# A hybrid decoder block on one core: 22 pairs of raw expert products ahead of the expert stage instead of 12, with the gate work in four pieces beside them

## The chip, the cores and the metric

The kernel runs on one core of one Trainium2 chip. The metric is device time in microseconds of one execution. Engines are named as in the profile: PE is TensorE, DVE is VectorE, ACT is ScalarE, POOL is GpSimd, SP is SyncE; PEld is the weight load of TensorE.

## What is computed

One decoder block for 256 tokens of width 2048, all in float32: adaLN modulation, two token mixers in parallel (sparse attention and an S5 state space), a merge, and then the expert mixer, in which most of the time goes. Cut to what the change touches:

```
mod = silu(c) @ ada_w + ada_b                # 6 parts of 2048: sh1, sc1, g1, sh2, sc2, g2
...
bu = einsum(u, bb)                           # S5: 64 groups of 16 channels drive a state of 64
x_re, x_im = associative_scan(...)           # y from the states
...
x  = x + g1 * (mixed @ w_out)
h2 = rms_norm(x) * (1 + sc2) + sh2
q  = h2 @ w_q                                # 8 heads, two halves of 128
s1, s2 = q @ sub_keys                        # top 16 of 128 twice, then top 16 of the sums
expert, gate = 16 of 16384 experts per head and token, softmax of their scores
x  = x + g2 * sum over (gate * gelu(h2 . u_tab[expert])) * v_tab[expert]
out = rms_norm(x) * final_g
```

The expert mixer is computed densely: h2 is multiplied with all 16384 rows of u, the result is multiplied with a gate matrix that is zero where an expert is not chosen, and that product is multiplied with all of v.

## The kernel before

All large matrix products are done three times over halves: `load_split` (L95 to L101) reads a block of 128x1024 into `st` (5 buffers, SP's queue), rounds it on ACT into `hi` (3 buffers) and subtracts on DVE into `lo` (3 buffers); PE multiplies hi with both halves of the other operand and lo with the first half. One such load is the unit of the whole kernel: one `st` transfer, one `hi` on ACT, one `lo` on DVE, 24 matmuls of 256 columns (or 12 of 512) on PE.

The program is written as one stream, and a scheduling layer places the instructions in fixed order on each engine. Work beside the main stream is put in with `tick`, which is called once for each load of `pair_T` and `cols_t`: it runs items of lists that have a first and a last load (`during`), and items of the list `later`, each with a cost in credits. A tick adds `credit[1]` (RATE, 2.0) to what is left of the credit, of which it keeps at most 2.0, and runs items from the head of `later` while the credit covers their cost:

```
credit[0] = min(credit[0], 2.0) + credit[1]
while later and later[0][0] <= credit[0]:
```

The stages in order are: the projections and mixers (to about 850 us), the second normalisation, and then from 882 us on, the part that the change is about:

- **Top-k scores.** Eight heads: a product of h2 with four blocks of w_q (`pair_T`), scores against the sub-keys (L1004), and top-k items into `later` (`top16`, `topk_head`, `topk_ranks`, `index`; L988 to L1062). Beside them `last` runs the final four column blocks of the adaLN matrix on PE (L222), one load per tick.
- **Raw products** (`u_raw`, L1144 on): a pair of expert blocks, 4 loads, 96 matmuls (L512 to L514), then a gelu in two ACT and two DVE instructions (L1149 to L1152) into an `xs` buffer (17 of them). `lead` = 12 pairs run before the gates exist.
- **Gates** (`gate_step`, L1109 on): 16 steps of 16 tokens. A step is four DVE instructions on 128x2048 (L1118 a comparison, L1120 twice a product, L1122 a comparison), 32 matmuls (L1128) and four ACT copies into `stage` (L1129). Two steps fill a chunk, which POOL's queue writes to `gt_dram`. `gate_step` costs 4.5 credits. What is left of `later` after the 12 pairs runs in a loop (L1229).
- **Expert stage**: 16 groups (q) of 8 expert blocks. `gate_load` reads a group's gates back (`gm`, 3 buffers, POOL's queue). `u_fin` multiplies raw values with them (L1159) and splits the result into `wcat` (3 buffers of four blocks, L104 and L105). `v_cols` (4 per group) multiplies with four blocks of v: 48 matmuls of 512 columns (L1180 to L1182), 64 `v_cols` in all. The other 52 pairs of raw products stand between them: two beside the `v_cols` of a group and two after its last.
- **End**: modulation by g2, residual, norm, output.

Two places further ahead are touched as well. `s5_state` (L578) starts each of 32 states with two products of 32 rows into one bank of PSUM (L590); `compress` (L673) multiplies 128 columns that are taken at a step of 8 (L682). PSUM has two banks named `mm` and six named `ps`.

Of the kernel before, what the change touches and what calls it, by code (L numbers as in the profile page):

```python
# [39 lines left out]
T8 = 2048 + 16  # L40
# [14 lines left out]
RATE = 2.0  # L55
# [17 lines left out]
def hybrid_block(ctx: ExitStack, tc: tile.TileContext, i: dict, out: bass.AP):  # L73
# [54 lines left out]
    pool = pa.enter_context(tc.tile_pool(name="pa", bufs=1))  # L128

    def t8(shape, name, dtype=F32):  # L130
        n = math.prod(shape[1:])
        t = pool.tile([P, T8], dtype, name=name, tag="t8", bufs=10)[:, :n]
        if len(shape) == 2:
            return t
        names = "abc"[:len(shape) - 1]
        return t.rearrange(f"p ({' '.join(names)}) -> p {' '.join(names)}", **dict(zip(names, shape[1:])))
# [420 lines left out]
    s5_out = {}  # L557

# [19 lines left out]
    def s5_state(b):  # L578

        cb, r = b // 4, b % 4  # L580
        if r == 0:
            if cb + 1 < 8:
                make_table(cb + 1)
            s5_mats(cb)
            s5_ps[cb] = ps_bank([P, SEQ])
        bst = s5_mat[cb][0]
        bu = ps2()
        sl = slice(32 * r, 32 * r + 32)
        for c in range(2):
            PE.matmul(bu[:, c], bst[sl, c, :], uT[sl, cb, :], start=True, stop=True)  # L590
# [82 lines left out]
    def compress(kind):  # L673
        xc = xcs[kind]
        pts = [ps_bank([P, P]) for _ in range(2)]
# [286 lines left out]
    NXS = 17  # L962
# [103 lines left out]
    last = [step for j in range(20, 24) for step in ada_steps(j, pl=tk)]  # L1066
    during(loads[0], loads[0] + 4 * PH, last)
# [6 lines left out]
    ada_row(1, 80, tk)  # L1074
# [28 lines left out]
    later.append((4.0, softmax))  # L1103
# [5 lines left out]
    def gate_step(t0):  # L1109

        if "stage" not in gpool:
            gpool["stage"] = pg.enter_context(tc.tile_pool(name="gp2", bufs=1))
        c, z = t0 // GT, t0 % GT
        if z == 0:
            chunk[c] = gpool["stage"].tile([P, NBLK, GT], F32, name="stage", bufs=2)
        ts = slice(t0, t0 + TG)
        o1 = gp.tile([P, 2, P, TG], HF, name="o1", bufs=2)
        V.tensor_tensor(o1[:, 0], iota_b, idxT[:, 0, None, ts].to_broadcast([P, P, TG]), op=OP.is_equal)  # L1118
        for part in (1, 0):
            V.tensor_mul(o1[:, part], o1[:, 0], gate2[:, part, None, ts].to_broadcast([P, P, TG]))  # L1120
        o2 = gp.tile([P, TG, P], HF, name="o2", bufs=2)
        V.tensor_tensor(o2, iota_r[:, None, :].to_broadcast([P, TG, P]),  # L1122
# [111 lines left out]
    for q in range(2):  # L1234
        gate_load(q)
# [132 lines left out]
```

## Time and profile before

| | |
|---|---|
| median of 3 runs (lowest, highest) | 2552.22 us (2546.16, 2557.81) |
| the profiled execution | 2554.16 us, of it 2552.1 us span |
| mean granted TensorE clock | 0.981 |
| busy: PE, DVE, ACT, POOL | 96%, 65%, 46%, 3% |
| HBM | 526.12 MB read, 23.12 MB written |

Busy shares are means over stages with different limits, and a pipelined matmul counts as busy from its issue to its modelled end, so a PE at 96% is not one at its peak. The pitch of its matmuls (the distance of two starts) tells more. In the slices of the page the span is cut into 40 pieces of 63.8 us; a digit is the busy share in tenths.

### The profile page before, as it was taken

How to read it: one execution, taken by the hardware profiler on the slowest of the kernel's cores; microseconds unless marked ns; L12 is line 12 of the kernel's file. 1: busy time of each engine (PE TensorE's matmuls, PEld its weight loads, DVE VectorE, ACT ScalarE, POOL GpSimd, SP SyncE). 2: the span in 40 equal slices, each digit the busy share in tenths (PEclk: the TensorE clock that was granted, in tenths of full speed). 3: DMA queues.
4: the chain of work that ended last, by engine and by line, in shares of the span. 5: the costliest groups of instructions: out<-in, count | busy, mean ns of one | idle time of the engine just before them, and what ended most of it. 6: DMA issues, size and time to landing. Idle time of an engine off the chain costs nothing.

```text
span 2552.1 us, 42825 instructions
## 1 busy us (share of the span) xinstructions
PE 2448.5 (96%) x17410; PEld 2127.0 (83%) x17410; DVE 1668.6 (65%) x2690; ACT 1176.5 (46%) x1527; POOL 65.1 (3%) x117
## 2 busy tenths in 40 slices
PE   7999999999999999995599999999999999999997
PEld 4787787777898788995488999999899999989996
DVE  4559767886555579959555665666666566665666
ACT  4444524645534534456444444444444444444444
POOL 0000200000000000000100000000000000000000
PEclk9999999999999999996799999999999999999999
DMA  9965666666777677554756665665666566565554
GB/s 347 376 227 176 225 202 210 214 199 209 281 264 255 211 237 253 188 186 173 298 197 192 211 198 197 203 208 191 203 206 207 192 204 206 191 207 189 190 191 139
DMA packets 149761, 552.03 MB, mean 216 GB/s; under 512 B 16748, under 2 KB 20492, under 8 KB 147133
## 3 DMA queue, kind: packets, MB, share of 16 engines
q1 hardware_dynamic: 135200, 493.08, 57.1%
q0 software_dynamic: 8928, 40.17, 4.4%
q10 hardware_dynamic: 5436, 16.06, 1.8%
q8 instruction: 136, 2.23, 0.4%
q14 instruction: 61, 0.49, 0.1%
HBM read 526.12 MB, written 23.12 MB: 215 GB/s over the span
## 4 chain that ended last, share of the span: by engine, by line
PE 57%; DVE 5%; DMA 2%; ACT 1%; issue 1%; DVEq 0%; POOL 0%; POOLq 0%; ACTq 0%
PE mm L512 10%; PE mm L513 10%; PE mm L514 10%; PE ps L1182 9%; PE ps L1180 9%; PE ps L1181 9%; DVE o L1120 1%; DVE o L1122 1%; DMA st<-in_peer_w_q_dram 1%; DVE lo L100 1%; DVE o L1118 1%; DMA gm<-gt_dram 0%; ACT hi L98 0%; PE ps L1004 0%; DMA gt_dram<-stage 0%
## 5 line engine op out<-in xcount | busy, mean ns | idle before, releaser
L100 DVE TENSOR_TENSOR lo<-st,hi 128x1024 fp32r<-128x1024 f32 x738 | 902.2, 1223 | 667.9 <-ACT hi L98 666.8
L98 ACT ACTIVATE hi<-st 128x1024 fp32r<-128x1024 f32 x738 | 781.4, 1060 | 1120.3 <-PE mm L513 430.5
L512 PE MATMUL mm<-cat,hi 128*128 128x256 f32 x2832 | 804.1, 284 | 0.6 <-ACT cat L104 0.6
L513 PE MATMUL mm<-cat,hi 128*128 128x256 f32 x2832 | 793.8, 280 | 1.0 <-DVE cat L105 0.9
L514 PE MATMUL mm<-cat,lo 128*128 128x256 f32 x2832 | 792.8, 280 | 0.0
L512 PEld LDWEIGHTS mm<-cat,hi 128*128 128x128 f32 x2832 | 533.6, 188 | 33.4 <-issue 26.5
L514 PEld LDWEIGHTS mm<-cat,lo 128*128 128x128 f32 x2832 | 539.6, 191 | 1.6 <-issue 0.8
L513 PEld LDWEIGHTS mm<-cat,hi 128*128 128x128 f32 x2832 | 533.5, 188 | 5.9 <-issue 2.4
L1180 PE MATMUL ps<-hi,wcat 128*128 128x512 f32 x1024 | 401.7, 392 | 21.0 <-ACT wcat L104 21.0
L1182 PE MATMUL ps<-hi,wcat 128*128 128x512 f32 x1024 | 403.0, 394 | 0.2 <-DVE wcat L105 0.2
L1181 PE MATMUL ps<-lo,wcat 128*128 128x512 f32 x1024 | 401.3, 392 | 0.0
L1180 PEld LDWEIGHTS ps<-hi,wcat 128*128 128x128 f32 x1024 | 193.1, 189 | 60.7 <-ACT wcat L104 21.1
L1182 PEld LDWEIGHTS ps<-hi,wcat 128*128 128x128 f32 x1024 | 192.9, 188 | 46.4 <-DVE wcat L105 4.8
L1181 PEld LDWEIGHTS ps<-lo,wcat 128*128 128x128 f32 x1024 | 193.2, 189 | 40.6
L431 PE MATMUL ps<-cat,hi 128*128 128x256 f32 x384 | 110.9, 292 | 0.5 <-ACT hi L98 0.5
L433 PE MATMUL ps<-cat,lo 128*128 128x256 f32 x384 | 106.8, 284 | 1.0 <-DVE lo L100 1.0
L432 PE MATMUL ps<-cat,hi 128*128 128x256 f32 x384 | 107.3, 281 | 0.1
L222 PE MATMUL ps<-st,sct 128*32 128x256 f32 x960 | 88.8, 390 | 0.4 <-DMA st<-in_ada_w_dram 0.4
L431 PEld LDWEIGHTS ps<-cat,hi 128*128 128x128 f32 x384 | 72.7, 190 | 16.0 <-issue 12.6
L1128 PE MATMUL ps<-o,o 128*128 128x128 f16 x512 | 49.5, 281 | 38.1 <-DVE o L1120 38.0
L1128 PEld LDWEIGHTS <-o 128*128 128x128 f16 x512 | 46.5, 159 | 41.0 <-DVE o L1120 40.8
L433 PEld LDWEIGHTS ps<-cat,lo 128*128 128x128 f32 x384 | 71.9, 190 | 4.5 <-DVE lo L100 2.0
(353 smaller groups left out, 2606.3 us busy)
## 6 DMA issues: line engine op xcount, KB each, us to landing
st<-in_peer_u_dram SPq DMA_DIRECT2D x256, 512.0 KB, 4.0
st<-in_peer_v_dram SPq DMA_DIRECT2D x256, 512.0 KB, 4.2
st<-in_ada_w_dram SPq DMA_DIRECT2D x136, 512.0 KB, 4.4
st<-in_w_in_dram SPq DMA_DIRECT2D x66, 512.0 KB, 4.0
ada_w<-in_ada_w_dram SPq DMA_DIRECT2D x28, 1024.0 KB, 9.5
st<-in_w_first_dram SPq DMA_DIRECT2D x48, 512.0 KB, 6.0
st<-in_w_out_dram SPq DMA_DIRECT2D x32, 512.0 KB, 4.0
st<-in_peer_w_q_dram SPq DMA_DIRECT2D x32, 512.0 KB, 4.3
```

Source lines behind the costliest of these rows:

```text
L98: S.activation(hi, st, AF.Copy)
L100: V.tensor_sub(lo, st, hi.bitcast(F32))
L431: PE.matmul(pt[:, e], hi[:, cs], hcat[:, k, 0], start=first, stop=False)
L432: PE.matmul(pt[:, e], hi[:, cs], hcat[:, k, 1], start=False, stop=False)
L433: PE.matmul(pt[:, e], lo[:, cs], hcat[:, k, 0], start=False, stop=end)
L512: PE.matmul(pt[:, e], wh, c[:, 0], start=(k == 0), stop=False)
L513: PE.matmul(pt[:, e], wh, c[:, 1], start=False, stop=False)
L514: PE.matmul(pt[:, e], wl, c[:, 0], start=False, stop=(k == n - 1))
L1128: PE.matmul(pt[:, tt], o1[:, part, :, h0 + tt], o2[:, h0 + tt], start=(part == 0), stop=(part == 1))
L1180: PE.matmul(pts[tb], wc[:, 0, ts], vh, start=(eb == 0), stop=False)
L1181: PE.matmul(pts[tb], wc[:, 0, ts], vl, start=False, stop=False)
L1182: PE.matmul(pts[tb], wc[:, 1, ts], vh, start=False, stop=(eb == GRP - 1))
```

## The change

- `lead` is 22 instead of 12; `xs` has 24 buffers instead of 17. RATE is 1.5 instead of 2.0, and the softmax costs 3.0 instead of 4.0.
- `gate_step` becomes `gate_steps`, four items of 1.0, 1.0, 1.0 and 1.8 credits: the first comparison, the two products, and the second comparison with matmuls, copies and the write.
- The final four column blocks of the adaLN matrix leave the top-k stage. They are read in another layout (`ada_r`) and multiplied on DVE, two instructions of 128x512 for each of 32 loads, one load beside each `v_cols`; PE only transposes the four sums (`ada_rows`).
- In the expert stage a pair of raw products and its `u_fin` stand before each `v_cols`. `gm` has 2 buffers instead of 3, `wcat` 4 of 8192 bytes instead of 3 of 8320; g2 and final_g lie in `xs` buffers.
- `s5_inputs` issues the products of two states together, alternating between two groups of 32 rows and two banks of PSUM.
- `compress` multiplies 80 columns instead of 128.
- The large buffers of the first part (`t8`) are 8192 bytes instead of 8256, so that all start at the same place modulo 512 bytes.

```
-RATE = 2.0
+RATE = 1.5
...
-    def s5_state(b):
-
-        cb, r = b // 4, b % 4
-        if r == 0:
+    def s5_inputs(b):
+
+        cb, r0 = b // 4, b % 4
+        if r0 == 0:
...
-        bu = ps2()
-        sl = slice(32 * r, 32 * r + 32)
+        bus = [ps2() for _ in range(2)]
         for c in range(2):
-            PE.matmul(bu[:, c], bst[sl, c, :], uT[sl, cb, :], start=True, stop=True)
+            for e in range(2):
+                sl = slice(32 * (r0 + e), 32 * (r0 + e) + 32)
+                PE.matmul(bus[e][:, c], bst[sl, c, :], uT[sl, cb, :], start=True, stop=True)
...
-                mv = xc[:, :, j:j + 121:8]
+                mv = xc[:, 0:5, j:j + 121:8]
...
-    NXS = 17
+    NXS = 24
...
-    last = [step for j in range(20, 24) for step in ada_steps(j, pl=tk)]
-    during(loads[0], loads[0] + 4 * PH, last)
...
-    later.append((4.0, softmax))
+    later.append((3.0, softmax))
...
+        return [(1.0, first), (1.0, lambda: gated(1)), (1.0, lambda: gated(0)), (1.8, products)]
...
-        gmat[q] = gpool["gg"].tile([P, SEQ // GT, GRP, GT], F32, name="gm", bufs=3)
+        gmat[q] = gpool["gg"].tile([P, SEQ // GT, GRP, GT], F32, name="gm", bufs=2)
...
-            w = pool.tile([P, 4 * 2 * SEQ + 32], FR, name="wcat", bufs=3)[:, :8 * SEQ]
-            wcat[b // 4] = w.rearrange("p (b c t) -> p b c t", b=4, c=2)
+            wcat[b // 4] = gpool["gg"].tile([P, 4, 2, SEQ], FR, name="wcat", bufs=4)
...
+    def ada_rows(j):
...
+            for e in range(c == 0, 2):
+                V.scalar_tensor_tensor(t["acc"], st[:, e * 512:(e + 1) * 512], sct[:, 2 * c + e, 0:1], t["acc"],
+                                       op0=OP.mult, op1=OP.add)
...
-    lead = 12
-    later += [(4.5, lambda t=t: gate_step(t)) for t in range(0, SEQ, TG)]
+    lead = 22
+    for t in range(0, SEQ, TG):
+        later += gate_steps(t)
...
-            if nxt and dc % 2 == 1:
+            if nxt:
...
+            for step in rows[:1]:
+                step()
+                rows.pop(0)
             v_cols(q, dc)
-        for b in nxt:
-            if b not in raw:
-                u_raw(b)
-            u_fin(b)
```

Where the gates stand on DVE, at the end of the raw products ahead. Before (line numbers of the kernel before; `lo` belongs to a load, `sq` and `xs` to a pair, `o` to a gate step):

```order
L100 TENSOR_TENSOR lo<-st,hi 128x1024 x3
L1150 SCALAR_TENSOR_TENSOR sq<-sq,mm 128x512
L1118 TENSOR_TENSOR o_12491<-iota_b,idxT 128x2048
L1152 SCALAR_TENSOR_TENSOR xs<-sq,mm 128x512
L1120 TENSOR_TENSOR o_12491<-o_12491,gate_9093 128x2048
L1122 TENSOR_TENSOR o_12495<-iota_r,idxT 128x2048
L1120 TENSOR_TENSOR o_12491<-o_12491,gate_9093 128x2048
L1118 TENSOR_TENSOR o_12537<-iota_b,idxT 128x2048
L1122 TENSOR_TENSOR o_12541<-iota_r,idxT 128x2048
```

Two steps stand further ahead, and the other 14 in one piece from here on, with no `lo` between them. With the change, a stretch out of the middle of the 22 pairs, with buffer numbers (L99 is `lo`, L1124, L1127 and L1132 are the gate's instructions, L1163 and L1165 the pair's):

```order
L1124 TENSOR_TENSOR o1_11834<-iota_b_9095,idxT_9093 128x2048
L99 TENSOR_TENSOR lo_11840<-st_11836,hi_11838 128x1024
L1127 TENSOR_TENSOR o1_11834<-o1_11834,gate2_9094 128x2048
L99 TENSOR_TENSOR lo_11878<-st_11874,hi_11876 128x1024
L1127 TENSOR_TENSOR o1_11834<-o1_11834,gate2_9094 128x2048
L99 TENSOR_TENSOR lo_11909<-st_11905,hi_11907 128x1024
L1132 TENSOR_TENSOR o2_11935<-iota_r_9097,idxT_9093 128x2048
L1163 SCALAR_TENSOR_TENSOR sq_11868<-sq_11868,mm_11697 128x512
L1124 TENSOR_TENSOR o1_11977<-iota_b_9095,idxT_9093 128x2048
```

All 16 steps now stand between the loads of the 22 pairs; the last one is followed on PE by the matmuls of 9 more loads and then by the first `v_cols`.

The first use of gates that were read back, on DVE, with the change (buffer numbers shown: `gm_14184` is group 0, `gm_14186` group 1; L1172 multiplies, L104 is the split into `wcat`, L1216 and L1218 the modulation):

```order
L99 TENSOR_TENSOR lo_14056<-st_14052,hi_14054 128x1024
L1216 TENSOR_SCALAR ada_a_14215<-st_14213,sct_91 128x512
...
L99 TENSOR_TENSOR lo_14086<-st_14082,hi_14084 128x1024
L1172 SCALAR_TENSOR_TENSOR xs_10559<-xs_10559,gm_14184 128x256 x2
...
L1172 SCALAR_TENSOR_TENSOR xs_11051<-xs_11051,gm_14184 128x256 x2
L1163 SCALAR_TENSOR_TENSOR sq_14046<-sq_14046,mm_13924 128x512
L1172 SCALAR_TENSOR_TENSOR xs_11213<-xs_11213,gm_14186 128x256
L99 TENSOR_TENSOR lo_14116<-st_14112,hi_14114 128x1024
L99 TENSOR_TENSOR lo_14146<-st_14142,hi_14144 128x1024
```

Before, these multiplications stood behind the last gate step with no load's `lo` behind them that a raw product waits for. Now the `lo` of the last two of the 88 loads stand behind them.

The state inputs on PE, before:

```order
L432 MATMUL ps_2058<-cat_180,hi_2054 128x256
L433 MATMUL ps_2058<-cat_180,lo_2056 128x256
L590 MATMUL ps_2112<-uT_1896,bst_2097 128x256 x2
L431 MATMUL ps_2131<-cat_180,hi_2127 128x256
L432 MATMUL ps_2131<-cat_180,hi_2127 128x256
```

and with the change, where L426 to L428 are the lines of the other matmuls, L587 is the state input, and ps_2113 and ps_2114 are two banks:

```order
L427 MATMUL ps_2059<-cat_181,hi_2055 128x256
L428 MATMUL ps_2059<-cat_181,lo_2057 128x256
L587 MATMUL ps_2113<-uT_1897,bst_2098 128x256
L587 MATMUL ps_2114<-uT_1897,bst_2098 128x256
...
L426 MATMUL ps_2135<-cat_181,hi_2131 128x256
```

One visit per state has become one visit per two states, and in it the two banks take turns (the two instructions shown come twice).

## Rows read from the trace of the kernel before

**Rows 1.** From the page: busy us of each engine (share of the span) with instruction counts, and the rows of PE and of the granted clock in 40 slices of the span.

```profile
PE 2448.5 (96%) x17410; PEld 2127.0 (83%) x17410; DVE 1668.6 (65%) x2690; ACT 1176.5 (46%) x1527; POOL 65.1 (3%) x117
...
PE   7999999999999999995599999999999999999997
...
PEclk9999999999999999996799999999999999999999
```

**Rows 2.** Busy time of each engine in stretches of 64 us: start and end, length, then PE, PEld, DVE, ACT and POOL (with instruction counts), granted clock, DMA share, GB/s.

```profile
192.00:256.00 64.00, 63.86 (x434) 47.58 (x432) 57.70 (x100) 30.62 (x39) 2.16 (x4) 1.00 0.54 180
...
1152.00:1216.00 64.00, 36.11 (x352) 33.76 (x352) 64.00 (x47) 42.63 (x44) 3.23 (x6) 0.69 0.47 196
...
1664.00:1728.00 64.00, 64.00 (x424) 58.36 (x423) 41.07 (x48) 30.83 (x36) 0.88 (x1) 1.00 0.62 207
```

**Rows 3.** PE's instructions in order of time at four places: start, length, line, operation, count, and the idle time before. The first two stand around the gates, the third and fourth at the end of them.

```profile
882.21 0.38 PE L512 MATMUL mm<-cat,hi 128*128 128x256 f32 x1 [0.64 <-ACT cat L104]
...
1142.46 4.25 PE L1128 MATMUL ps<-o,o 128*128 128x128 f16 x60
...
1209.73 2.21 PE L1128 MATMUL ps<-o,o 128*128 128x128 f16 x32 [1.10 <-DVE o L1120]
...
1226.68 3.39 PE L1128 MATMUL ps<-o,o 128*128 128x128 f16 x32 [3.49 <-DVE o L1120]
1251.04 0.80 PE L1180 MATMUL ps<-hi,wcat 128*128 128x512 f32 x1 [20.97 <-ACT wcat L104]
```

**Rows 4.** DVE in order of time at the last gate step and after it.

```profile
1221.95 2.28 DVE L1122 TENSOR_TENSOR o<-iota_r,idxT 128x2048 f16<-128x2048 f16 x1
1224.15 2.47 DVE L1120 TENSOR_TENSOR o<-o,gate 128x2048 f16<-128x2048 f16 x2
1249.56 2.10 DVE L1159 SCALAR_TENSOR_TENSOR xs<-xs,gm 128x256 f32<-128x256 f32 x6 [22.94 <-DMA gm<-gt_dram]
```

**Rows 5.** DMA issues by line: size and median time from issue to landing.

```profile
gt_dram<-stage POOLq DMA_DIRECT2D x8, 2048.0 KB, 6.6
gm<-gt_dram POOLq DMA_DIRECT2D x16, 1024.0 KB, 10.1
```

**Rows 6.** PE in the expert stage, in order of time: the first matmul of a piece each, and the last of the stage. From L512 to L1180 is one pair of raw products (96 matmuls), from L1180 to L512 two `v_cols` (96 matmuls).

```profile
1363.78 0.39 PE L1180 MATMUL ps<-hi,wcat 128*128 128x512 f32 x1
...
1385.88 0.28 PE L512 MATMUL mm<-cat,hi 128*128 128x256 f32 x1
...
1440.72 0.28 PE L512 MATMUL mm<-cat,hi 128*128 128x256 f32 x1
...
1451.61 0.39 PE L1180 MATMUL ps<-hi,wcat 128*128 128x512 f32 x1
...
1473.38 0.28 PE L512 MATMUL mm<-cat,hi 128*128 128x256 f32 x1
...
1484.69 0.39 PE L1180 MATMUL ps<-hi,wcat 128*128 128x512 f32 x1
...
2538.88 0.39 PE L1182 MATMUL ps<-hi,wcat 128*128 128x512 f32 x1
```

**Rows 7.** Groups of instructions from 960 to 1149 us: line, operation, shapes, count, busy us, mean ns of one, idle time of the engine before them. The first five are DVE's, the last PE's.

```profile
L100 DVE TENSOR_TENSOR lo<-st,hi 128x1024 fp32r<-128x1024 f32 x62 | 75.5, 1218 | 30.8 <-ACT hi L98 30.7
L1150 DVE SCALAR_TENSOR_TENSOR sq<-sq,mm 128x512 f32<-128x512 f32 x12 | 8.1, 679 | 0.0
L1120 DVE TENSOR_TENSOR o<-o,gate 128x2048 f16<-128x2048 f16 x4 | 4.9, 1213 | 0.0
L1122 DVE TENSOR_TENSOR o<-iota_r,idxT 128x2048 f16<-128x2048 f16 x2 | 4.6, 2281 | 0.0
L1118 DVE TENSOR_TENSOR o<-iota_b,idxT 128x2048 f16<-128x2048 f16 x3 | 3.6, 1216 | 0.0
...
L1128 PE MATMUL ps<-o,o 128*128 128x128 f16 x64 | 4.4, 226 | 0.1
```

**Rows 8.** Busy time from the first top-k instruction to the drain of the gates (columns as in rows 2), and the same stretch for the instructions of L100 on DVE alone.

```profile
894.00:1142.40 248.40, 242.13 (x2096) 227.79 (x2095) 201.99 (x622) 102.42 (x119) 0.52 (x1) 0.99 0.66 218
...
894.00:1142.40 248.40, 91.28 (x75) 0.99 0.66 218
```

**Rows 9.** What PE waited for from 882 to 1149 us (total, times, longest).

```profile
PE ps L1004 <- ACT qs L999: 6.3, 6, 3.3
```

**Rows 10.** PE in order of time at a state input, at an attention score (two groups of 64 rows in turn) and at the compression, each with the row behind it.

```profile
304.82 1.13 PE L590 MATMUL ps<-uT,bst 32*128 32x256 f32 x4
305.88 0.64 PE L222 MATMUL ps<-st,sct 128*32 128x256 f32 x8
...
313.71 7.82 PE L682 MATMUL ps<-xc,st 128*128 128x128 f32 x33
321.17 0.48 PE L512 MATMUL mm<-cat,hi 128*128 128x256 f32 x1
...
490.06 1.14 PE L791 MATMUL ps<-kT,qT 64*128 64x256 f32 x8
491.12 0.38 PE L512 MATMUL mm<-cat,hi 128*128 128x256 f32 x1
```

**Rows 11.** Counts of the matmul records of both lines from 190 to 600 us (columns as in rows 7).

```profile
L590 PE MATMUL ps<-uT,bst 32*128 32x256 f32 x128 | 36.5, 402 | 0.0
L682 PE MATMUL ps<-xc,st 128*128 128x128 f32 x128 | 30.2, 413 | 0.0
```

More of the change, by code (lines that the diff above doesn't have):

```diff
@@ L674, in compress @@
         xc = xcs[kind]
-        pts = [ps_bank([P, P]) for _ in range(2)]
+        pts = [ps_bank([P, 80]) for _ in range(2)]
         for c in range(4):
@@ new lines, in gate_steps, with first, gated @@
+        t = {}
+        def first():
+            if "stage" not in gpool:
+                gpool["stage"] = pg.enter_context(tc.tile_pool(name="gp2", bufs=1))
+            if z == 0:
+                chunk[c] = gpool["stage"].tile([P, NBLK, GT], F32, name="stage", bufs=2)
+            t["o1"] = gp.tile([P, 2, P, TG], HF, name="o1", bufs=2)
+            V.tensor_tensor(t["o1"][:, 0], iota_b, idxT[:, 0, None, ts].to_broadcast([P, P, TG]), op=OP.is_equal)
+        def gated(part):
+            V.tensor_mul(t["o1"][:, part], t["o1"][:, 0], gate2[:, part, None, ts].to_broadcast([P, P, TG]))
@@ new lines, in products @@
+        def products():
+            o1 = t["o1"]
+            o2 = gp.tile([P, TG, P], HF, name="o2", bufs=2)
+            V.tensor_tensor(o2, iota_r[:, None, :].to_broadcast([P, TG, P]),
+                            idxT[:, 1, ts, None].to_broadcast([P, TG, P]), op=OP.is_equal)
+            for h0 in range(0, TG, 4):
+                pt = ps_bank([P, 4, P])
+                for tt in range(4):
+                    for part in range(2):
+                        PE.matmul(pt[:, tt], o1[:, part, :, h0 + tt], o2[:, h0 + tt],
+                                  start=(part == 0), stop=(part == 1))
+                S.activation(chunk[c][:, :, z + h0:z + h0 + 4].rearrange("p e t -> p t e"), pt, AF.Copy)
+            if z + TG == GT:
+                G.dma_start(gt_dram[c], chunk.pop(c))
@@ L1193, in hybrid_block, with products, columns @@
     fin = {}
+    def ada_rows(j):
+        t = {}
+        def products(c):
+            st = load(i["ada_r"][j - 20, c])
+            if c == 0:
+                t["acc"] = pool.tile([P, 512], F32, name="ada_a", bufs=1)
+                V.tensor_scalar(t["acc"], st[:, :512], sct[:, 0, 0:1], None, op0=OP.mult)
+            for e in range(c == 0, 2):
+                V.scalar_tensor_tensor(t["acc"], st[:, e * 512:(e + 1) * 512], sct[:, 2 * c + e, 0:1], t["acc"],
+                                       op0=OP.mult, op1=OP.add)
+        def columns():
+            pt = ps_bank([P, 4, P])
+            for c in range(4):
+                PE.transpose(pt[:, c], t["acc"][:, c * P:(c + 1) * P], ident)
+            s4 = pool.tile([P, 4], F32, name="ada_5", bufs=2)
+            V.tensor_reduce(s4, pt, axis=AX.X, op=OP.add)
+            V.tensor_add(modT[:, 4 * j:4 * j + 4], s4, adab[:, 4 * j:4 * j + 4])
+        return [lambda c=c: products(c) for c in range(8)] + [columns]
+    rows = [step for j in range(20, 24) for step in ada_rows(j)] + [lambda: ada_row(1, 80, pool)]
     def residual():
-        x3 = gpool["gg"].tile([P, 4 * D], F32, name="x3")
-        fin["x"] = x3[:, 0:2 * D].rearrange("p (t d) -> p t d", t=TB)
-        fin["g2"] = x3[:, 2 * D:3 * D]
-        fin["fg"] = x3[:, 3 * D:4 * D]
+        fin["x"] = gpool["gg"].tile([P, TB, D], F32, name="x3")
         fin["ss"] = pool.tile([P, TB, 4], F32, name="ss4")
```

56 lines of the change are left out of this document (22 added, 34 removed).

## The prediction

> **What bounds the kernel now.** First the page: PE is busy 96% of the span, and two of its 40 slices alone fall to 5, where the granted clock falls as well [rows 1]. So PE is the bound nearly everywhere, and one place is not like the rest. The stretches of 64 us show it: from 1152 to 1216 us DVE is busy for the whole 64.00 us, PE for 36.11, and the granted clock is 0.69, while in a stretch of the expert stage PE has 64.00 and DVE 41.07 [rows 2]. PE's order of time names the place [rows 3]: at 1142.46 the raw products ahead are done, gate matmuls follow, each behind DVE, and the first `v_cols` starts at 1251.04 after an idle time of 20.97. DVE's last gate instruction ends at 1226.62, and its next instruction waits 22.94 us for `gm` [rows 4], which lies behind a write of 6.6 us and a read of 10.1 us [rows 5]. The reader is to see two things in these 108.6 us: 14 gate steps on DVE with PE hardly used, then 23 us in which every engine waits for a round trip through memory. On both sides the kernel is bound by the pitch of matmuls.
>
> **Prices.** A pair of raw products takes 10.89 us (1440.72 to 1451.61) or 11.31 (1473.38 to 1484.69); both occur, and I take 11.1, or 2.775 a load. Two `v_cols` take 21.77 (1451.61 to 1473.38), in another group 22.10 (1363.78 to 1385.88) [rows 6]. The 32 matmuls of a gate step have taken 2.21 us back to back [rows 3]. On DVE a gate step costs 1.22 + 2 x 1.21 + 2.28 = 5.9 us, a load 1.22, a pair 2 x 0.68 [rows 7].
>
> **Ahead of 882 us.** State inputs: 128 records in 32 visits [rows 11] of 1.06 us (304.82 to 305.88) [rows 10], 33.9 us together. Now a visit serves two states in alternating row groups. The nearest row is the attention score, which alternates between two groups of 64 rows: eight records in 1.06 us (490.06 to 491.12), as long as four here [rows 10]. So 16 visits of 1.06: 17.0 us saved, or nothing if groups of 32 rows don't run side by side. The Trainium skill (TensorEngine Tiling (Array Packing), Restrictions and Gotchas) says against it that row tiling raises the pressure on PSUM, since different row tiles write different banks. By that rule up to these 17 us would go in waits for a bank, by the row none; no row of before shows such a pair of 32 rows, and it is the second rival. Compression: 33 records take 7.46 us (313.71 to 321.17), 0.226 each [rows 10], 128 of them 28.9 us [rows 11]. With 80 columns of 128 that is 18.1: 10.8 us saved if time goes with columns, nothing if it does not; I take the first, since columns are all that is taken away. DVE is busy 57.70 of 64 us where the states begin [rows 2], so I give 2 us back. The equal starts of the large buffers I count as nothing: their products are few. Sum **-26**, between -11 and -28.
>
> **From 882.2 us to the first `v_cols`**, 368.8 us before [rows 3]. PE's part up to 1142.46 is 260.3: 80 loads are 222.0, and 38.3 remain. Of these the adaLN loads leave, 32 visits of some 0.55 us (eight records at L222 were busy 0.64, the end of the last one included [rows 10]), 17.6 in all; two gate steps are 4.4; 16.3 stay, 6.3 of it PE waiting for `qs` [rows 9]. After: 120 loads are 333.0, 16 gate steps 35.4, and 16.3: 384.7.
>
> Does DVE keep up? From 894 to 1142.4 us it was busy 201.99 us, with 75 instructions of `lo` among it [rows 8], 11 pairs and 2 gate steps. Up to the last gate instruction the new order has 105, 18 and 16: 30 x 1.22 + 7 x 1.36 + 14 x 5.9 = 129 more, 331 us. PE needs for the same stretch 384.7 less the 11.8 before 894 us and the 9 loads behind the last gate step (25): 348. DVE would be 95% busy. In the trace, PE did not wait while gate matmuls stood between loads (0.1 us idle before 64 of them [rows 7]). I put **7 us** on this tightness, between 0 and 35.
>
> The round trip is now behind raw products. From the end of the last gate matmuls (1226.68 + 3.39) to the first multiplication (1249.56) it takes 19.5 us [rows 3, 4]. PE has 9 loads to do, but the `lo` of the last two stand on DVE behind the multiplications, so seven cover: 19.4. The `lo` comes after nine multiplications of 0.35 [rows 4], one instruction of a pair and itself, 5.1 us. So PE waits about **5 us**, between 0 (DVE early) and 15 (transfers slowed by the loads beside them). Sum: 384.7 + 7 + 5 = 396.7, against 368.8: **+28**.
>
> **Expert stage**, 1251.04 to 2538.88 [rows 6]. Ten pairs fewer: -111. The two speeds of `v_cols`: the three `wcat` buffers lie 8320 bytes apart, so they start at three different places modulo 512, and a group uses two of them in turn; a difference of 0.33 in two `v_cols` fits one slow buffer, which two groups of three use, 40 `v_cols` of 0.165 or 6.6 us. The new buffers start all alike: I take them as fast, like two of three, -6.6; if all are slow, it is +14. The first matmul was busy 0.80 us and later ones 0.39 [rows 3, 6], at a granted clock below full; without the idle time ahead that is gone, -3. On PE 16 transposes come in, +2. On DVE the modulation costs 64 instructions of 0.68 (L1150 has the same shape [rows 7]), 44 us in 37 steps; one step beside a `v_cols` of 10.9 us makes, with four `lo`, two additions, two multiplications and a split, about 9, so it is hidden at 83%. Its 32 transfers only move. With two `gm` buffers the order multiplies groups 3 to 5 a few instructions after the buffer they need is released: about three loads (8.3 us) stand against a read of 10.1 and its issue, three times, some 8 us, of which PE's two loads in hand cover most: +3, between 0 and 9. Sum **-116**. The end is unchanged.
>
> **Total.** -26 + 28 - 116 = -114. The profiled execution took 2554.2 us, so 2440; it stood 2 us above the median, and I say **2439**.
>
> **The rivals.**
> 1. *VectorE sets the pace of the products ahead.* It is 95% planned, and its order is fixed: what waits for ACT or PE in it delays every `lo` behind. At 85% its 331 us become 389, the last gate step ends at 1283 instead of about 1249, and the kernel takes 2439 + 34 = **2473**. For it: DVE was busy 202 of 248 us though work was there [rows 8]. Against it: PE hardly waited there [rows 9]. Chance 0.20.
> 2. *Two banks held for each pair of states.* PE waits for DVE to empty them, and the 17 us do not come; with the compression unchanged too, all 26 are lost: **2465**. For it: DVE's 90% in that place [rows 2]. By the rule on PSUM pressure this is where it would show. Against it: a state holds its bank only for two DVE multiplications. Chance 0.10.
> 3. *PE stands at the gate matmuls.* They are now in PE's order between loads, and PE does not pass them. If each step waits for its last product on DVE, 16 waits replace one. From 114 / 16 = 7.1 us a step the kernel is slower than before; at 9 us it takes 2439 + 144 = **2583**. For it: PE idled 3.49 and 1.10 us before such steps where DVE was full [rows 3]. Against it: 0.1 us where loads stood between [rows 7]. Chance 0.03.
> 4. *The buffers don't do what they are for*: all `wcat` starts are slow, the 6.6 us stay and 14 come on top: **2460**. Chance 0.05.
> 5. *Everything overlaps better*: no wait at the round trip, DVE early, raw products mostly at 10.89: 72 pairs x 0.2 and 12 us less give **2413**. Chance 0.07.
>
> My forecast keeps 0.55. It spreads by the bounds of its own terms, some 20 us to either side, so cases 1, 2 and 4 lie at its upper end. The range **2415 to 2480** takes them in and leaves out case 3, half of case 5 and the worst of case 1. A measurement of this kernel can tell about 0.5%, 13 us, from no change. Only case 3, and the sum of several bad ends, reaches that or worse: faster 0.95, the same 0.02, slower 0.03.
>
> **What would show it.** Right: the granted clock stays at full from 960 to 1280 us; the first `v_cols` starts near 1253 us with no more than some 10 us idle before it; a state visit holds eight records in about 1.06 us, compression records come every 0.14; all `v_cols` take 10.89; DVE is above 90% through the products ahead. Wrong: long waits of PE on `lo` from 890 to 1250 us (case 1), on a bank at the state inputs (case 2) or on the gate's products (case 3); `v_cols` at 11.05 or more; a first `v_cols` later than 1280.

## The result, and the profile after

The change takes 2457.73 us (median of 4 runs, 2456.87 to 2460.36) against 2550.76 us for the kernel before (4 runs), a ratio of 0.9635 with a 95% interval of [0.9611, 0.9659]. The forecast was 2439 us in 2415 to 2480. The sign, the place and the main mechanism came as predicted; the time is 19 us above the forecast, and several terms of the sum were off. The profiled execution took 2457.3 us, its span 2455.5.

From the page of the kernel after, the lines that answer to [rows 1]: the dent in PE and in the granted clock is gone but for one slice at 7.

```profile
PE 2380.5 (97%) x17154; PEld 2090.2 (85%) x17154; DVE 1699.8 (69%) x2754; ACT 1175.6 (48%) x1525; POOL 65.0 (3%) x117
...
PE   7999999999999999999979999999999999999997
...
PEclk9999999999999999999999999999999999999999
```

Stretches of 64 us of the kernel after, columns as in [rows 2]. In the third line, where the hole was, PE now has 64.00 with DVE at 54.29. The fourth and fifth are new: PE at 52.13 and 57.94, with the DMA engines at 0.87 and 0.72. In the first, PE is 4 us short of what it had before.

```profile
192.00:256.00 64.00, 59.61 (x432) 47.27 (x431) 57.82 (x103) 31.57 (x39) 2.62 (x5) 0.97 0.53 177
512.00:576.00 64.00, 62.83 (x544) 51.70 (x543) 46.70 (x89) 29.25 (x62) 0.00 (x0) 0.97 0.60 199
1152.00:1216.00 64.00, 64.00 (x646) 63.79 (x646) 54.29 (x48) 47.21 (x53) 1.60 (x3) 1.00 0.73 256
1216.00:1280.00 64.00, 52.13 (x318) 46.22 (x317) 43.66 (x69) 29.14 (x38) 4.99 (x6) 0.92 0.87 313
1280.00:1344.00 64.00, 57.94 (x245) 46.80 (x246) 41.71 (x55) 26.28 (x30) 1.77 (x2) 0.97 0.72 245
1664.00:1728.00 64.00, 64.00 (x412) 58.39 (x411) 43.10 (x51) 29.06 (x32) 0.88 (x1) 1.00 0.71 236
```

PE in order of time, kernel after, columns as in [rows 3]. In turn: a visit of two states (8 records, 1.06 us) and 64 compression records (9.34 us, 0.146 each), against [rows 10]; the last transposes of h2; a gate step between loads; the wait of 9.82 us for the round trip, and the first `v_cols` (L1192), against [rows 3]; one pair (L507 to L1192, 11.31 us) and one `v_cols` (L1192 to L507, 10.88 us), against [rows 6]; a wait of 3.33 us near the end; the last matmul of the stage.

```profile
303.50 1.13 PE L587 MATMUL ps<-uT,bst 32*128 32x256 f32 x8
304.56 0.64 PE L217 MATMUL ps<-st,sct 128*32 128x256 f32 x8
305.13 9.61 PE L688 MATMUL ps<-xc,st 128*128 128x80 f32 x64
314.47 0.40 PE L507 MATMUL mm<-cat,hi 128*128 128x256 f32 x1
...
856.31 0.44 PE L183 MATMUL ps<-ident,xn 128*128 128x128 f32 x2
...
1190.86 2.22 PE L1138 MATMUL ps<-o,o 128*128 128x128 f16 x32
...
1243.33 0.58 PE L509 MATMUL mm<-cat,lo 128*128 128x256 f32 x1 [9.82 <-DVE lo L99]
...
1250.15 0.39 PE L1192 MATMUL ps<-hi,wcat 128*128 128x512 f32 x1
...
1459.19 0.28 PE L507 MATMUL mm<-cat,hi 128*128 128x256 f32 x1
...
1470.50 0.39 PE L1192 MATMUL ps<-hi,wcat 128*128 128x512 f32 x1
...
1481.38 0.28 PE L507 MATMUL mm<-cat,hi 128*128 128x256 f32 x1
...
2329.57 0.58 PE L509 MATMUL mm<-cat,lo 128*128 128x256 f32 x1 [3.33 <-DVE lo L99]
...
2441.77 0.39 PE L1194 MATMUL ps<-hi,wcat 128*128 128x512 f32 x1
```

The kernel before had its last transposes here, 23.6 us later:

```profile
879.87 0.44 PE L188 MATMUL ps<-ident,xn 128*128 128x128 f32 x2
```

So the difference of the spans, 96.6 us, divides like this: up to the last transposes of h2 -23.6 (the forecast took 882.2 as the border and said -26), from there to the first `v_cols` +22.7 (+28), expert stage 1287.8 to 1191.6, -96.2 (-116), end +0.5 (0).

The first of these parts is the least certain. The change and ten of the kernels below have the same instructions up to the last transposes of h2, and in their profiled executions the last of these starts anywhere from 851.4 to 860.8 us (856.5 in the change). From there to the end of the expert stage, the change, `lead_24` and `states_single` (whose edits change nothing in that stretch's sum) took 1585.2 to 1585.3 us. So a few us in a total show little by themselves, and the stretch in which an edit acts is the firmer comparison.

DVE in order of time, kernel after, at the start of the expert stage. The first row is the first multiplication with `gm`, behind an idle time of 7.72 us for which the profile names no releaser (in `lead_24`, below, the same place has 11.25 and names `gm`); the others are steps of the modulation that stand idle for their load, each with the `lo` of the next loads behind it.

```profile
1238.17 2.77 DVE L1172 SCALAR_TENSOR_TENSOR xs<-xs,gm 128x256 f32<-128x256 f32 x8 [7.72 <-issue]
...
1274.53 0.75 DVE L1218 SCALAR_TENSOR_TENSOR ada_a<-st,sct,ada_a 128x512 f32<-128x512 f32 x1 [3.99 <-DMA st<-in_ada_r_dram]
...
1288.71 0.75 DVE L1218 SCALAR_TENSOR_TENSOR ada_a<-st,sct,ada_a 128x512 f32<-128x512 f32 x1 [3.19 <-DMA st<-in_ada_r_dram]
...
1303.87 0.75 DVE L1218 SCALAR_TENSOR_TENSOR ada_a<-st,sct,ada_a 128x512 f32<-128x512 f32 x1 [5.21 <-DMA st<-in_ada_r_dram]
```

ACT in order of time, kernel after, ahead of the wait at 2329.57 (`ACTq` is ACT issuing transfers): two more issues of `g2` at 2321.35, four of `final_g`, and then three `hi` in a row that had been due before.

```profile
2321.35 0.81 ACTq L1242 DMA_DIRECT2D g<-g_dram  x2
2322.20 2.32 ACTq L1242 DMA_DIRECT2D fg<-in_final_g_dram  x4
2324.62 2.95 ACT L97 ACTIVATE hi<-st 128x1024 fp32r<-128x1024 f32 x3 [2.64 <-DMA g<-g_dram]
```

### The profile page after: what moved, and what is told of

Same layout as the page of the kernel before. It is cut to its first block, busy times and chain, and to the rows that moved or that the text cites. A ratio compares the mean times of both kernels' runs of the same rounds, so it can differ in the third digit from the quotient of the medians.

```text
span 2455.5 us, 42391 instructions
## 1 busy us (share of the span) xinstructions
PE 2380.5 (97%) x17154; PEld 2090.2 (85%) x17154; DVE 1699.8 (69%) x2754; ACT 1175.6 (48%) x1525; POOL 65.0 (3%) x117
## 5 line engine op out<-in xcount | busy, mean ns | idle before, releaser
L99 DVE TENSOR_TENSOR lo<-st,hi 128x1024 fp32r<-128x1024 f32 x738 | 900.8, 1223 | 514.6 <-ACT hi L97 513.7
L507 PE MATMUL mm<-cat,hi 128*128 128x256 f32 x2832 | 802.7, 283 | 0.7 <-ACT cat L103 0.7
L507 PEld LDWEIGHTS mm<-cat,hi 128*128 128x128 f32 x2832 | 536.1, 189 | 20.8 <-issue 13.4
L1192 PE MATMUL ps<-hi,wcat 128*128 128x512 f32 x1024 | 399.4, 390 | 0.0
L1192 PEld LDWEIGHTS ps<-hi,wcat 128*128 128x128 f32 x1024 | 192.5, 188 | 38.5
L426 PE MATMUL ps<-cat,hi 128*128 128x256 f32 x384 | 111.2, 292 | 1.2 <-ACT hi L97 1.2
L428 PE MATMUL ps<-cat,lo 128*128 128x256 f32 x384 | 107.5, 285 | 3.6 <-DVE lo L99 3.6
L426 PEld LDWEIGHTS ps<-cat,hi 128*128 128x128 f32 x384 | 73.3, 192 | 15.9 <-issue 11.5
L428 PEld LDWEIGHTS ps<-cat,lo 128*128 128x128 f32 x384 | 72.6, 191 | 8.0 <-DVE lo L99 5.4
L427 PEld LDWEIGHTS ps<-cat,hi 128*128 128x128 f32 x384 | 73.3, 191 | 1.9 <-issue 1.6
L1202 DVE TENSOR_TENSOR acc<-acc,ps 128x512 f32<-128x512 f32 x112 | 73.3, 682 | 1.7 <-PE ps L1194 1.7
L1218 DVE SCALAR_TENSOR_TENSOR ada_a<-st,sct,ada_a 128x512 f32<-128x512 f32 x60 | 45.0, 750 | 42.3 <-DMA st<-in_ada_r_dram 41.5
```

Source lines behind the costliest of these rows:

```text
L99: V.tensor_sub(lo, st, hi.bitcast(F32))
L426: PE.matmul(pt[:, e], hi[:, cs], hcat[:, k, 0], start=first, stop=False)
L427: PE.matmul(pt[:, e], hi[:, cs], hcat[:, k, 1], start=False, stop=False)
L428: PE.matmul(pt[:, e], lo[:, cs], hcat[:, k, 0], start=False, stop=end)
L507: PE.matmul(pt[:, e], wh, c[:, 0], start=(k == 0), stop=False)
L1192: PE.matmul(pts[tb], wc[:, 0, ts], vh, start=(eb == 0), stop=False)
```

## The experiments

Each is the kernel after with the edit shown. The times are medians of 4 or 5 runs; stage times come from the profiled executions. PE's waits in a stretch are summed from its matmuls' starts: what lies between two starts beyond the 0.227 or 0.118 us of a matmul; such sums come out somewhat above the idle times in the lines. The experiments ask what the gain is made of, where the 19 us went, and whether the waits that are left can be taken away. Line numbers past an edit shift by its length, so L1192 of the change (the first product of `v_cols`) is L1195 or L1196 in some.

### What the gain is made of

**22 pairs, whole gate steps** (`whole_22`).

```
-RATE = 1.5
+RATE = 2.0
...
-        return [(1.0, first), (1.0, lambda: gated(1)), (1.0, lambda: gated(0)), (1.8, products)]
+        return [(4.5, whole)]          # whole() runs the four in turn
```

> The change with each gate step whole, at the cost of 4.5 and with the credit of 2.0 a load of before; 22 pairs ahead as in the change. Since credit is capped at 4.0, no whole step can start beside a load. Theory: the 22 pairs alone hide nothing, the 16 steps stand behind them with the 108.6 us of before, less the 32 us that their matmuls take in the change and the 10 us of its round trip: about 2525 us. Rival: the pairs ahead are what hides the work, and the pieces only smooth it: 2460 to 2495 us.

Measured: 2520.16 us, ratio to the kernel before 0.988 [0.9855, 0.9906]; 62 us slower than the change. In PE's order of time all 16 steps stand behind the loads again, and from the first gate matmul to the first `v_cols` it takes 108.3 us, as long as the hole before.

```profile
1216.33 4.51 PE L1138 MATMUL ps<-o,o 128*128 128x128 f16 x64
1227.53 3.63 PE L1138 MATMUL ps<-o,o 128*128 128x128 f16 x32 [6.69 <-DVE o L1127]
...
1324.63 0.80 PE L1196 MATMUL ps<-hi,wcat 128*128 128x512 f32 x1 [20.57 <-ACT wcat L103]
```

The raw products ahead hide nothing when no gate step can start beside them; the pieces, small enough for the credit, are what puts the gate work beside them. The theory holds, the rival falls.

**Pieces, but 12 pairs** (`lead_12`).

```
-RATE = 1.5
+RATE = 2.0
...
-    lead = 22
+    lead = 12
```

> The change with 12 pairs ahead instead of 22 and the credit of 2.0 for a load, both as before; the pieces of the gate work and all else stay as in the change. Theory (my main term): of the 97 us gained most is the gate work of VectorE that lies beside raw products. With 12 pairs the stretch from 857 us to the first v_cols is some 351 us instead of 393 (before's 368.8 less the 17.6 of modulation loads), with the hole of about 100 us in it again, and ten pairs of 11.3 us come back into the expert stage: about 2525 us. Rival: the pairs ahead only move work, and the gain is the work taken off PE (state inputs, compression, modulation): about 2465 us.

Measured: 2496.28 us, 0.9796 [0.9777, 0.9815]; 39 us slower than the change, where 67 were expected. Both theories miss. In pieces, 12 of the 16 steps went beside the 80 loads, since DVE has time there that the whole steps, too dear for the credit, could not use; PE paid with short waits, and then 24.54 us for the round trip with nothing to do:

```profile
1021.13 3.42 PE L1138 MATMUL ps<-o,o 128*128 128x128 f16 x32 [2.14 <-DVE o L1127]
...
1182.18 0.79 PE L1192 MATMUL ps<-hi,wcat 128*128 128x512 f32 x1 [24.54 <-ACT wcat L103]
```

So with 22 pairs the pieces are worth 62 us, and with pieces the ten further pairs are worth 39. Of these, 14.7 are the round trip (24.54 against 9.82), and PE's waits for the gate's products are another 13.5 (14.5 us in all against 1.0); the rest was not taken apart.

**The modulation back on PE** (`mod_on_pe`).

```
+    last = [step for j in range(20, 24) for step in ada_steps(j, pl=tk)]
+    during(loads[0], loads[0] + 4 * PH, last)
...
-    rows = [step for j in range(20, 24) for step in ada_rows(j)] + [lambda: ada_row(1, 80, pool)]
+    rows = []
...
```

> The last modulation is back on TensorE, beside the score stage, as before; all else as in the change. Theory: 17.6 us of PE's time come back, 1.4 of transposes go, and the 10.5 us that the start at the 17th v_cols saved are saved as well: about 2463 us. Rival (my prediction: the modulation costs nothing where it was put): 2474 us.

Measured: 2471.81 us, 0.9695 [0.9668, 0.9722]; 14 us slower than the change. The theory counted too little on PE: the first `v_cols` comes 28 us later (1278.0 against 1250.1), of which the 256 records at L217 are the largest part, in the groups from 850 to 1280 us:

```profile
L217 PE MATMUL ps<-st,sct 128*32 128x256 f32 x256 | 21.7, 390 | 0.0
```

In exchange the expert stage is 13 us shorter (1178.6 against 1191.6): on DVE the modulation is not hidden. My prediction's number for the total (2474) came near because two errors cancelled: the part gives 28 us ahead and takes 13 back.

**The state inputs one at a time** (`states_single`): `s5_state` as before the change, two products of one row group per visit.

> The inputs of a state are computed one state at a time again, as before. Theory: records of two row groups share their time, 16 us in all: about 2473 us. Rival: in the trace of the change PE has about 9 us of small waits between 190 and 600 us that before did not show, which eat half of it: about 2465 us.

Measured: 2461.14 us, 0.9658 [0.9642, 0.9674]; 3 us slower, and the intervals of the two kernels overlap, so that the size is uncertain. Neither number: the 128 records take 34.4 us from start to start here and 18.4 in the change, but of these 16 us some 13 are lost again. The records do share their time (1.06 us for eight, above). But in the same stretch the kernel with single states keeps PE busy, and DVE does the same 57.82 us of work in both:

```profile
192.00:256.00 64.00, 63.85 (x435) 47.71 (x433) 57.82 (x101) 30.85 (x39) 2.15 (x4) 1.00 0.52 182
```

With pairs, PE waits there for `lo`, `s_m` and `hi`, and up to 560 us for the transposes' `a_s` as well, some one us at a time, and the granted clock is 0.97 in two stretches. The largest such waits of the change from 185 to 700 us (total, times, longest):

```profile
PE ps L825 <- ACT a_s L817: 3.8, 5, 1.0
PE ps L428 <- DVE lo L99: 2.5, 2, 1.8
```

From 190 to 600 us PE is idle for 7 to 9 us in the change and in all the other kernels with pairs, and for 0.5 with single states. No wait named is for a bank. That DVE's work on two states now stands in a bunch ahead of a `lo` fits the waits named, but wasn't tested by itself.

### Where the 19 us went

**The modulation from the 17th `v_cols` on** (`rows_later`).

```
-            for step in rows[:1]:
+            for step in rows[:1] if 4 * q + dc >= 16 else []:
```

> The 37 steps of the modulation start at the 17th v_cols instead of the first (one step per v_cols, as in the change). In the trace of the change PE waits 12 us at v_cols of the first five groups, where no raw products stand between. Theory: VectorE stands there at a modulation step whose load has not come (18 times, 40 us), with the lo of the v_cols behind it. Then these waits fall to about 2 us and the kernel takes about 2447 us. Rival: the two gm buffers, whose multiplications stand ahead of the lo on VectorE: nothing changes there, the waits stay at 8 us or more, 2454 to 2458 us.

Measured: 2447.22 us, 0.9589 [0.9573, 0.9605]. The waits of the first groups fall from 12 us to 6, and the expert stage from 1191.6 to 1184.8 us. Up to the last transposes the two kernels have the same instructions; from there to the end of the stage the kernel is 6.6 us shorter, so not all of the 10.5 us between the medians is the edit's. What is left is mainly one wait, and it is the rival's: DVE stands at its 41st multiplication, the first of group 5, which the prediction had named with groups 3 and 4,

```profile
1278.47 1.09 DVE L1172 SCALAR_TENSOR_TENSOR xs<-xs,gm 128x256 f32<-128x256 f32 x3 [5.22 <-DMA gm<-gt_dram]
```

a wait that the change does not have: there the multiplications come later, behind the modulation's own waits. So both theories own a part, and the modulation the larger one.

**g2 and final_g on GpSimd's queue** (`g2_on_pool`).

```
-                nc.scalar.dma_start(fin[name][dc], src[:, dc * 512:(dc + 1) * 512].to_broadcast([P, 512]))
+                G.dma_start(fin[name][dc], src[:, dc * 512:(dc + 1) * 512].to_broadcast([P, 512]))
```

> The eight transfers of g2 and final_g ahead of the last group but one are issued by GpSimd instead of ScalarE. In the trace of the change PE waits 6.2 us at 2325 us. Theory: ScalarE stands at these issues until a buffer of xs comes free, and the hi of three loads behind it; then the 6.2 us go: about 2451.5 us. Rival: it is VectorE's work on the last-but-one sums (it needs g2) that holds the lo: the wait stays, 2457 us.

Measured: 2452.97 us, 0.9608 [0.9592, 0.9624]. PE waits for nothing between 2250 and 2420 us any more; the first groups had 15 us of waits in this execution, 3 more than in the change. The theory's outcome holds: with the issues gone from ACT, the wait is gone. Its reason does not. GpSimd issues the eight a hundred us earlier,

```profile
2214.58 2.16 POOL L1242 DMA_DIRECT2D g<-g_dram  x4
2216.72 1.59 POOL L1242 DMA_DIRECT2D fg<-in_final_g_dram  x3
2222.28 0.54 POOL L1242 DMA_DIRECT2D fg<-in_final_g_dram  x1 [3.96 <-DMA gm<-gt_dram]
```

so the buffers of the `xs` ring had long been free when ACT issued them at 2317 to 2324 us in the change. What ACT's rows show there is a split into `wcat` that waits 2.17 us for DVE's multiplication, and then six issues in a row, 3.1 us, ahead of the three `hi`. How the wait divides between the two was not tested.

**Half of the gated products at another start** (`odd_half_128`), and **all of them** (`all_128`).

```
+            odd = b // 4 % 2
+            if odd and "pad2" not in gpool:
+                gpool["pad2"] = gpool["gg"].tile([P, 96], F32, name="pad2")
-            wcat[b // 4] = gpool["gg"].tile([P, 4, 2, SEQ], FR, name="wcat", bufs=4)
+            wcat[b // 4] = gpool["gg"].tile([P, 4, 2, SEQ], FR, name="wodd" if odd else "wcat", bufs=2)
```

```
-    gpool["gg"].tile([P, 8], F32, name="pad")
+    gpool["gg"].tile([P, 104], F32, name="pad")
```

In the change all four buffers start 256 bytes past a multiple of 512. Both pads add 384 bytes, which makes 128 past the next multiple; the second moves everything behind it, `gm` too.

> The second half of each group's gated products lies 128 bytes past a multiple of 512 (buffers 3 and 4 of wcat), the first half as in the change. In the trace of before a matmul of v_cols took 0.232 us from such a start and 0.227 from the others, and the raw products behind a v_cols that ended at 0.232 came every 0.113 us, behind one that ended at 0.227 every 0.118; in the change all v_cols are at 0.227 and all 42 pairs at 0.118. Theory: the pace of a pair is set by the v_cols ahead of it. Then 1536 matmuls cost 0.005 us more, 8 us, and 42 pairs 0.42 us less, 17.5: about 2448 us, faster than the change though half of its alignment is undone. Rival: the pace of a pair has another cause; then only the 8 us come: 2466 us.

> All four wcat buffers lie 128 bytes past a multiple of 512. Theory of the linked pace: 3072 matmuls cost 0.005 us more, 15 to 16 us, and 42 pairs 0.42 less, 17.5: about 2456 us, no difference from the change. Rival (the pace of a pair has another cause): 2473 us, which would be what my prediction counted as all buffers slow.

Measured: 2446.64 us, 0.9595 [0.9579, 0.9611], for the half; 2467.75 us, 0.9678 [0.9662, 0.9694], for all. Groups of PE's matmuls from 1460 to 2300 us, columns as in [rows 7]: in the change a raw matmul is busy 281 ns and one of `v_cols` 389; with half of them moved, 276, and 390 or 396 by the buffer; with all moved, 281 and 394.

```profile
L507 PE MATMUL mm<-cat,hi 128*128 128x256 f32 x1214 | 341.1, 281 | 0.0
...
L1192 PE MATMUL ps<-hi,wcat 128*128 128x512 f32 x604 | 235.2, 389 | 0.0
```

```profile
L507 PE MATMUL mm<-cat,hi 128*128 128x256 f32 x1231 | 340.1, 276 | 0.0
...
L1195 PE MATMUL ps<-hi,wodd 128*128 128x512 f32 x304 | 120.3, 396 | 0.0
...
L1195 PE MATMUL ps<-hi,wcat 128*128 128x512 f32 x304 | 118.7, 390 | 0.0
```

```profile
L507 PE MATMUL mm<-cat,hi 128*128 128x256 f32 x1213 | 340.4, 281 | 0.0
L1193 PE MATMUL ps<-lo,wcat 128*128 128x512 f32 x593 | 233.9, 394 | 0.0
```

With the half, all 42 pairs come at 0.113 us a matmul and the stage is 9.2 us shorter, though 1536 matmuls are slower: the theory's 9.5. With all, 37 of 42 pairs stay at 0.118, against the theory in the words I gave it. What the two have apart is how a `v_cols` ends. Over the change, the kernel before and the experiments, a pair behind a `v_cols` whose last matmul took 0.231 us or more (from its start to the next) ran at 0.113 in 178 cases of 183; behind one whose last took less, at 0.118 in 397 of 399. Five pairs are left out, where PE stood still ahead of them; where it did so within a pair, the pace before that is taken. With all four buffers moved, most `v_cols` run at 0.232 but end on an interval of 0.226 or 0.227. So the pace of a pair goes with the last interval ahead of it. That the interval sets it is not shown: no run changes it alone, 161 of the 178 come from the four kernels in which the moved buffers end every `v_cols`, and in `all_128`, the kernel that tells the last interval from the buffer's start, only 3 of 7 pairs behind a slow interval are fast (2 of 35 behind the others). Why a pair keeps its pace, and why those `v_cols` end as they do, stays open.

### The waits that are left

**24 pairs ahead** (`lead_24`), edit `lead = 24`.

> 24 pairs ahead instead of 22, so that 17 loads instead of 9 stand behind the last gate step. Theory: the 10 us that PE waits at the end of the products ahead are the round trip, less the loads beside it; four loads more (11 us) fill them, and the kernel takes about 2448 us. Rival: the wait lies in the order of VectorE, where the lo stand behind multiplications that wait for gm, and it comes again behind the added loads, or as longer waits in the first five groups: 2455 to 2458 us.

Measured: 2454.19 us, 0.9634 [0.9615, 0.9653]; no difference that can be told from the change, and from the last transposes to the end of the stage both take 1585.3 us. The rival holds: with eight more loads' work to do, PE waits as long as ever, at the same time,

```profile
1243.39 0.58 PE L509 MATMUL mm<-cat,lo 128*128 128x256 f32 x1 [10.31 <-DVE lo L99]
```

because DVE stands at the first multiplication, and the `lo` of loads that have arrived are behind it in its order:

```profile
1238.50 2.77 DVE L1172 SCALAR_TENSOR_TENSOR xs<-xs,gm 128x256 f32<-128x256 f32 x8 [11.25 <-DMA gm<-gt_dram]
...
1242.12 2.36 DVE L99 TENSOR_TENSOR lo<-st,hi 128x1024 fp32r<-128x1024 f32 x2
```

**Four edits together** (`all_four`: `rows_later`, `g2_on_pool`, `odd_half_128`, `lead_24`).

> The change with the modulation from the 17th v_cols on, g2 and final_g on GpSimd's queue, the odd halves of the gated products at 128 past a multiple of 512, and 24 pairs ahead. If the four gains add up (10.5, 5, 11 and 9 to 10 us): about 2422 us. If they share the same waits in the first five groups, as the wait of 5.5 us for gm that came in place of the modulation's would have it: 2430 to 2435 us.

Measured: 2434.47 us, 0.9558 [0.9542, 0.9574]. The expert stage has 2.0 us of waits in all instead of 18.7, but the 10 us ahead of it stay: the fourth edit alone brings nothing. The number is the one of the second theory, by another way: it is the fourth gain that is missing, and the other three together, 26 us by their medians, are nearly all there (23).

**The multiplications held back** (`late_24`), on top of the four.

```
     for p in range(lead):
         u_raw(2 * p)
+        if p == lead - 2:
+            late = par("lam_re")[:, 0:1]
+            V.tensor_scalar(late, raw[2 * p][:, 0, 0:1], 0.0, 1.0 / GSC, op0=OP.mult, op1=OP.add)
+            fin["late"] = late
...
-            V.scalar_tensor_tensor(x3, x3, 1.0 / GSC, gmat[q][:, :, bl + e], op0=OP.mult, op1=OP.mult)
+            V.scalar_tensor_tensor(x3, x3, fin["late"] if q < 2 else 1.0 / GSC, gmat[q][:, :, bl + e], ...)
```

> The kernel with all four edits, and the first two groups' multiplications by gm take their factor from a cell that VectorE writes behind the last pair but one (the same value), so that they can't stand in VectorE's order ahead of the lo of these pairs. Theory after the run with 24 pairs: PE's 10 us at the round trip come from VectorE's order alone. Then they go and the kernel takes about 2424 us, 10 below the one with all four. Rival: the transfers themselves slow the loads there (the DMA engines are at 0.87 in that stretch): a wait of 5 us or more stays, 2430 us or more.

Measured: 2423.67 us (5 runs, 2421.25 to 2427.12), 0.9506 [0.9484, 0.9529]. The wait at the round trip is gone; the first multiplication now waits for the cell alone, `gm` being there,

```profile
1249.96 1.67 DVE L1172 SCALAR_TENSOR_TENSOR xs<-xs,small,gm 128x256 f32<-128x256 f32 x4 [0.26 <-DVE small L1272]
```

and the stretch in which the change had PE at 52.13 has

```profile
1216.00:1280.00 64.00, 61.69 (x435) 57.01 (x434) 47.17 (x71) 33.09 (x41) 4.46 (x5) 0.97 0.81 294
```

with the DMA engines at 0.81. So it was DVE's order, not the transfers, that made the 10 us. But 5 us of waiting come up further on: PE's waits inside the expert stage are 7.0 us, where the kernel with all four edits had 2.0, most of them at `v_cols` of the first groups:

```profile
PE ps L1196 <- DVE lo L99: 4.1, 3, 2.3
```

From the last transposes to the end of the stage the kernel is 6.9 us shorter than the one with all four; the rest of the 10.8 between the medians is not accounted for by the edit, and 4.9 us of the difference of the two profiled executions lie in the part that both have alike. The kernel is 34 us (1.4%) below the change.

**Only a quarter at the other start** (`late_pair`): tiles of two blocks, the last pair of a group in tiles at 128 past a multiple of 512.

> As the last kernel, but only the last pair of each group's gated products (one load of v_cols in four, 12 matmuls of 48) lies 128 past a multiple of 512, in tiles of two blocks. Theory: what sets the pace of a pair of raw products is how the last matmuls of the v_cols ahead of it run, so a quarter does as well as a half, and 768 matmuls cost 0.005 us less: about 2420 us, with 40 fast pairs of 40. Rival: after 12 matmuls from such a start the pairs fall to 0.118 us as they did where all four buffers lay there: 40 pairs cost 17 us more, about 2436 us.

Measured: 2424.91 us (5 runs, 2417.10 to 2429.59), 0.9494 [0.947, 0.9519]. All 40 pairs ran at 0.113 us, so 12 slower matmuls at the end of a `v_cols` do as well as 24, and the expert stage took 1149.7 us against 1151.3. The total can't be told from the kernel ahead of it: in its profiled execution the stages up to the last transposes of h2 took 9 us more.

## Why the prediction was right, and which terms were not

**What bounds.** Right: the hole and the round trip were 108.6 us in which nothing needed PE to stand, and pieces of gate work beside raw products fill them. `whole_22` brings the hole back to the microsecond.

**Ahead of 882 us, -26: right in sum, wrong in its parts, so luck.** The compression is as said (0.146 us a record, 10.8 saved). The state inputs, -17, are worth some 3: the row price of 1.06 for eight was right, but where I gave 2 us back for VectorE, some 13 went. The second rival had the outcome, and named DVE's 90% for it; but its mechanism, a bank held, does not show. (The Trainium skill, TensorEngine Tiling (Array Packing), Restrictions and Gotchas, has row tiling raise the pressure on PSUM. By that rule PE would wait at L587; the trace does not bear this out, its waits are for `lo`, `s_m`, `hi` and `a_s`.) What filled the gap I had at nothing or had missed: summed from start to start, the products with the large buffers of the attention and state outputs fell by some 5 us (whether by their equal starts, no run undoes), and 40 adaLN records, 3.7 us, stood ahead of 882 us.

**From there to the first `v_cols`, +28: 5 too many.** VectorE kept up, as the forecast had it and the first rival not: from 896 to 1216 us it was busy 301 of 320 us, 94%, and PE was short of it by 5 us. Two slips of mine nearly cancel: the two gate steps (4.4) that I took out of PE's work of before are not in it, since a step of 4.5 never fits under a credit of 4.0; and the loads took 2.72 us where I had 2.775, 6.6 in all. The same misreading is in my evidence: the 64 gate matmuls of [rows 7] are those of 1142.46 in [rows 3], behind the last load and not between loads, so they could tell nothing on PE's waits there, neither for the 7 us nor against the third rival. And the 6.3 us for `qs`, which I left in the sum, are gone: the change has no such wait. The round trip is 9.8 us, where I had 5 in a range of 0 to 15. I had seen that `lo` would stand behind the multiplications; `lead_24` and `late_24` show that this order makes the wait; what I had too low is its price. The third rival falls: PE waited 1.0 us in all for the gate's products. The fifth falls by the waits above. Of the signs that I named, one failed: the granted clock did not stay at full up to 1280 us, it was 0.92 in the stretch from 1216 with the wait in it.

**Expert stage, -116: 20 too much, and here the miss lies.** Summed from start to start, the raw products fell by 105.2 us and the `v_cols` by 6.2, the transposes added 1.4, and PE's waits rose from 5.0 to 18.7. I had counted nothing for waits in sum (-3 and +3): these 13.7 us are the larger part of the miss.
- Ten pairs, -111, measured -105. Before, 14 of the 39 stretches of raw products in this stage (a pair or two each) ran at 0.113; after, none of 42.
- Buffer starts, -6.6: the `v_cols` all come at 10.88 us, as said, and save 6 us; but where the `v_cols` became fast, the pairs behind them went to 0.118, a link that `odd_half_128` bears out. The two nearly cancel. The fourth rival falls in its words.
- Modulation, hidden at 83% of VectorE: mis-sized at 0. It costs 7 us of the stage by `rows_later`, which moves it back, and 13 by `mod_on_pe`, which takes it away. The share was right and the wrong question: not DVE's work but its standing still for a load, with `lo` behind, made PE wait (`rows_later`).
- The two `gm` buffers, +3 between 0 and 9: not seen in the change, where the modulation's waits lie over them; 5.5 us once that is moved.
- Not in the sum: the end's vectors, issued by ACT ahead of three `hi`, 6.4 us of PE (`g2_on_pool`).
- Transposes, +2: 1.4.

## What to carry to other kernels

In these traces an instruction that waits for a transfer held up everything behind it on its engine, however idle that engine was: a busy share of 70 or 80% says nothing on it, so ask of each moved instruction what its order has behind it when its data are late. More work ahead of such a place helps only if its own inputs don't stand behind it; holding the waiting instruction back took away 10 us of waiting, 5 of which came up again further on, where two more pairs of work took away nothing. And undo each part of a change by itself, even when the sum came out: here one part was worth a fifth of its price and another gave half of its gain back.

## What the runs showed that I had not expected

- Matmuls with the same operands and places ran at one of two paces, 0.113 or 0.118 us for 256 columns, for a whole pair of 96, and which of them went with whether the matmul ahead of the pair had taken 0.231 us or more (575 of 582 pairs). With faster `v_cols` the pairs behind them were slower; a quarter of slower `v_cols` matmuls, the last, was enough to keep the pairs fast. The cause is open.
- A stationary operand at 128 bytes past a multiple of 512 made a matmul of 512 columns take 0.232 us instead of 0.227 (`all_128`, `odd_half_128`).
- Sharing the array between two row groups halved the matmuls' time as the trace has it (18.4 us instead of 34.4 for 128 records) and moved the kernel by some 3 us.
